# The last two gate cells of a decoder trunk: products in an order of their own, one sum in PSUM, and a closing scale on two engines

## The chip, the cores and the metric

The kernel runs on one core of one Trainium2 chip. The core's engines work side by side, each with its own queue in fixed order: PE (matrix products, with its weight loads beside them), DVE (elementwise), ACT (functions and copies), POOL (small scalar steps here) and SP, which issues the DMAs. The metric is the device time of one execution in microseconds (us), taken as the median of several runs.

## What is computed

The reference is one decoder layer over a sequence of 1024 rows of 1024 columns, in float32, with a gated linear attention branch, a short convolution branch, a merge, an output projection, a gated per-layer embedding and a final norm. The change concerns its end only:

```
ple_gate = sigmoid(rms_norm(x, norm_ple_g) @ w_ple_gate)
x = x + ple_gate * (p @ w_ple_proj)
return rms_norm(x, norm_final_g)
```

The product p @ w_ple_proj is made at the start of the kernel and kept in DRAM (`ped`). The norm ahead of the gate is folded into the weight (its gain) and into the sigmoid's scale (`rgate`, one value per row). So what is left at the end is a matrix product of x with the gate's weight, the sigmoid, a multiplication by `ped`, an addition to x, and the final norm: the mean square of each row, its power of -0.5 (`rf`), and a multiplication by `rf` and by the gain `gf`.

## The kernel before

**Cells.** Every large product is cut into cells. A gate cell `gt0` to `gt3` makes 256 rows of the gate; its operands are halved both ways, and instead of eight products of the halves it makes seven by the Strassen-Winograd scheme (class `Cell`, line 704). Each product is twelve matmuls: four steps of 128 along the inner dimension, and each step three times, since a float32 operand is split into a high and a low part (`mm3`, line 591). A product accumulates in a PSUM bank of 128 x 512. A cell has three banks: X, Y and V. Two cells make a pair, with banks m0 to m2 for the first and m3 to m5 for the second.

With p0 to p6 for the products, the four quarters of a cell's result come out like this (`run`, line 763):

- quarter (0,0) is X = p0 + p3
- Y begins as a copy of p0 (ACT), and becomes U2 = p0 + p2. Product 2 is followed by an ACT copy of Y into SBUF (`c12`)
- V = p1, copied by ACT into SBUF (`c22`)
- quarter (0,1) is V + p5 + c12: product 5 runs on into V, and then DVE adds V and c12 (line 788)
- quarter (1,1) is U2 + p4 + c22: product 4 runs on into Y, then DVE adds Y and c22 (line 792)
- quarter (1,0) is U2 + p4 + p6: product 6 runs on into Y

For the very last cell product 6 is made in two halves of 256 columns (`last_product`, line 748): the first goes on in Y, the second in another bank Z, into which ACT has copied Y before. This lets the first half be read while the second is made. Z is here the X bank of the other cell.

**Order.** A pair takes turns: product 0 of the first cell, product 0 of the second, then 1, 2, 3, 5, 4 and 6 in the same manner (`PAIR`, line 702; `line_up`, line 802). The matmuls of products are put on PE in just this order. `run_groups` (line 816) prepares the streamed operand of a product (`prep`: sums and differences on DVE, the split by an ACT cast and a DVE subtraction) seven products ahead, in a ring of eight buffers, and loads its parts fourteen products ahead.

**The queues.** The program first notes all operations, and a planner (class `Flow`, line 247) then sorts them. `set_dues` gives every operation a due time, counted back from the end with a cost and a latency for each kind of operation. `put_in_order` runs a model of the five queues: at each step it takes the engine that can start soonest, and on it, of the operations that are ready by then, the one with the earliest due. `hurry` moves a due by hand. The order so found is the fixed order of each queue; on the chip an operation that isn't ready holds what stands behind it.

**The end of a gate cell.** `make_gate` (line 1637) says what happens to each quarter. In the usual way (`cons`, line 1688) there are the sigmoid (ACT), the product with `pe` (DVE), the addition to x (DVE) and the mean square (ACT with an accumulator). After both quarters of a row block POOL makes `rf` in two steps, and one DVE operation over 1024 columns multiplies by `rf` and `gf`; one store follows. The second row block of gt2 and of gt3 goes through `piece` (line 1643): the quarter that comes first is already multiplied by `gf`, and when the last piece is there, `rf` is made by an addition on DVE and a power on POOL. Then the first quarter is only scaled by `rf` and stored, and the last one is multiplied by `rf` and `gf` and stored. For gt2 the scale of 512 columns is on DVE; for gt3 512 columns are scaled by ACT and 256 by DVE. All stores are issued by SP. The rows of x that gt2 and gt3 need are loaded into four buffers (tag "x", line 1684) that the row blocks of gt0 and gt1 hold until they are stored.

Of the kernel before, what the change touches and what calls it, by code (L numbers as in the profile page):

```python
# [9 lines left out]
F32 = mybir.dt.float32  # L10
# [6 lines left out]
P = 128  # L17
# [229 lines left out]
class Flow:  # L247
# [12 lines left out]
    def note(self, engine, op, call, args, kw):  # L260
# [12 lines left out]
        for d in shape[1:]:  # L273
            n *= d
        o.lat = 0.15
        if engine == PE:
# [127 lines left out]
    def put_in_order(self):  # L404
# [28 lines left out]
        while len(order) < len(ops):  # L433
            best = None
            for e in range(5):
                found = [(max(clock[e], w), n) for n in waiting[e] for w in [since(ops[n])] if w is not None]
                first = None
                if e == PE and at < len(main) and not ops[main[at]].left:
                    w = since(ops[main[at]])
                    if w is not None:  # L440
                        first = (max(clock[e], w), main[at])
                when = min([w for w, _ in found + ([first] if first else [])], default=None)
                if when is None or best and best[0] <= when:
                    continue
                ripe = [n for w, n in found if w <= when]
                pick = min(ripe, key=lambda n: (ops[n].due + (6.0 if ops[n].table and ops[n].table != table else 0.0), n),
                           default=None)
                best = (when, e, first[1] if pick is None else pick)
            assert best, "nothing can run"
            when, e, n = best  # L450
            o = ops[n]
# [45 lines left out]
BACKLOG = 3.0  # L497
LATE = 2.2
START = 30.0


@with_exitstack
def kernel(
# [195 lines left out]

    ORDER, PAIR = tuple(range(7)), (0, 1, 2, 3, 5, 4, 6)

    class Cell:


        def __init__(self, name, side, src, res, cons, prods=ORDER, begin=None, s1=None, u2=None, s5=None, fresh=()):
            self.name, self.side, self.src, self.res, self.cons = name, side, src, res, cons
            self.prods, self.begin, self.after = list(prods), begin, None
            self.get = {"u2": u2, "s5": s5}  # L710
            self.s1, self.seed, self.ready, self.halves = s1, None, lambda k: True, None
# [11 lines left out]

        def prep(self, k):
            if k not in self.ring:
                self.load(k)
                self.ring[k] = self.steps[k]()

# [18 lines left out]

        def last_product(self):

            other = psm.tile([P, 512], F32, tag=f"m{3 * (1 - self.set)}", name=f"{self.name}Z")  # L750
            nc.scalar.copy(other, self.Y)
            self.prep(6)
            shi, slo = self.ring[6]
            rhi, rlo = self.res[6]
# [8 lines left out]
        def run(self, k):  # L763
            if k == self.prods[0]:
                if self.begin:
                    self.begin()
                self.Y = None
            if k == 0:
                self.X = bank(self, 0)
                self.product(0, self.X, True)  # L770
# [2 lines left out]
            elif k == 1:  # L773
# [3 lines left out]
                self.V = bank(self, 2)  # L777
                self.product(1, self.V, True)
                self.c22 = self.taken("s5", self.V)
            elif k == 2:  # L780
                self.product(2, self.Y, False)
                self.c12 = self.taken("u2", self.Y)
            elif k == 3:
                self.product(3, self.X, False)
                self.cons(0, 0, self.X)
            elif k == 5:
                self.product(5, self.V, False)
                tt(self.c12, self.V, self.c12, op=ALU.add)
# [13 lines left out]
    def line_up(groups):  # L802
        for n, g in enumerate(groups):
            for s, c in enumerate(g):
                c.set = (s if len(g) > 1 else n) % 2
        return [(c, k) for g in groups for k in g[0].prods for c in g]

    def single(cs):
        return [[c] for c in cs]

    def pairs(cs):
        for c in cs:
# [759 lines left out]
    with phase("late", [ph["sw"], ep]) as lp:  # L1572
# [60 lines left out]
        with phase("fin", [ph["sw4"]], lp) as gp:  # L1633
# [3 lines left out]
            def make_gate(p, cell):  # L1637
# [3 lines left out]


                def piece(i, cs, src, n, done):
                    w = cs.stop - cs.start
                    a = cs.start
# [8 lines left out]
                    act(junk[:, 0:w], xc, AF.Square, scale=1.0 / 32.0, accum_out=m)  # L1654
                    if not done:
                        tt(xc, xc, gf[:, cs], op=ALU.mult)
                        pre = gp.tile([P, 1], F32, tag="pre", name=f"pre{p}_{i}_{n}", bufs=4)
# [12 lines left out]
                    if a:  # L1670
                        nc.vector.tensor_scalar(xt[i][:, 0:a], xt[i][:, 0:a], r[:, 0:1], None, op0=ALU.mult)
                    store(out[rows(2 * p + i), 0:512], xt[i][:, 0:512])

                def late_cons(i, j, src):
                    if not xt:
                        get()
                    piece(i, slice(512 * j, 512 * j + 512), src, 1 - j, j == 0)

                def halves(n, src):
                    piece(1, slice(256 * n, 256 * n + 256), src, 1 + n, n == 1)  # L1680
# [25 lines left out]
                cell.cons = cons  # L1706
# [73 lines left out]
```

## Time and profile before

| | |
|---|---|
| median of 3 runs | 1102.06 us (1101.98 to 1102.79) |
| the profiled execution | 1102.23 us |
| its span in the profile | 1100.4 us |
| granted PE clock | 0.998 of full speed |
| instructions | 15273, of them 5050 matmuls |
| PE, DVE, ACT, POOL busy | 99%, 78%, 54%, 5% of the span |

A timeline row has the start in us from the beginning of the span, the duration, the engine, the line of the program, the operation, the tiles (out <- in, without their numbers), the shapes and the count of merged instructions; a bracket at its end gives the idle time before it and what ended that. All lines of computing read L491, since the planner issues everything from there; so tiles tell the steps apart: gt3Y is bank Y of gt3, `junk` the mean square, `pe` the product of gate and embedding, `x` the row block, `rf` the closing factor. In a row of the windows view stand the stretch, its length, and for each engine its busy time and in brackets its instructions (PE, PE's weight loads, DVE, ACT, POOL), then the granted clock, the share of the 16 DMA engines and GB/s. A row of waits has who waited, for whom, the total in us, how often, and the longest.

### The profile page before, as it was taken

The page shows a single profiled execution, that of the slowest core. Times are in us where ns is not written, and L with a number is a line of the kernel's source. Part 1 is how long each engine was busy: PE and PEld are TensorE (multiplying, and loading weights), DVE is VectorE, ACT ScalarE, POOL GpSimd, SP SyncE. Part 2 cuts the span into 40 slices and gives each one's busy share as a digit, 9 for nine tenths or more (in the row PEclk, how much of TensorE's full clock was granted, in tenths as well). Part 3 has the DMA queues.
Part 4 walks back from the last instruction along what each step waited for, and adds up shares of the span by engine and source line. Part 5 has one row for each costly group of instructions (what it writes and reads, how often), then busy time and mean ns, then how long its engine had stood idle before and what let it go on. Part 6 is the DMA issues. An engine that isn't in the chain of part 4 may idle for free.

```text
span 1100.4 us, 15273 instructions
## 1 busy us (share of the span) xinstructions
PE 1089.4 (99%) x5050; PEld 908.3 (83%) x5050; DVE 855.8 (78%) x1386; ACT 598.2 (54%) x1107; POOL 56.0 (5%) x116
## 2 busy tenths in 40 slices
PE   9999999999999999999999999999999999999996
PEld 7888888788888888888888898888888888888885
DVE  6996477789878878748649587876999889868666
ACT  6775347866543554343333377766736445457554
POOL 0000000000000000000000022230000000002021
PEclk9999999999999999999999999999999999999999
DMA  9957463358867595222212699988595888889653
GB/s 317 327 184 246 131 210 109 117 172 252 255 221 268 177 313 180 88 66 66 87 58 65 220 307 345 323 267 293 207 308 176 301 260 291 293 311 320 238 201 114
DMA packets 152574, 238.94 MB, mean 217 GB/s; under 512 B 12976, under 2 KB 66480, under 8 KB 149424
## 3 DMA queue, kind: packets, MB, share of 16 engines
q1 hardware_dynamic: 152496, 237.98, 65.0%
q8 instruction: 39, 0.64, 0.2%
q14 instruction: 39, 0.32, 0.1%
HBM read 157.19 MB, written 80.74 MB: 216 GB/s over the span
## 4 chain that ended last, share of the span: by engine, by line
PE 96%; ACT 2%; DVE 2%; issue 0%; POOL 0%; DVEq 0%; ACTq 0%
PE vacc L491 7%; PE op L491 3%; PE pe L491 2%; PE X L491 2%; PE ga2Y L491 1%; PE ga3Y L491 1%; PE ga1Y L491 1%; PE ga0Y L491 1%; PE out1Y L491 1%; PE gc1Y L491 1%; PE out0Y L491 1%; PE gc0Y L491 1%; PE out3Y L491 1%; PE out2Y L491 1%; PE za0Y L491 1%; PE xc3Y L491 1%
## 5 line engine op out<-in xcount | busy, mean ns | idle before, releaser
L491 ACT ACTIVATE junk<-x 128x512 bf16<-128x512 f32 (+1 forms) x29 | 17.8, 615 | 12.0 <-DVE x L491 11.5
L491 ACT ACT_TABLE_LOAD x17 | 21.8, 1283 | 3.4 <-issue 2.4
L491 DVE TENSOR_TENSOR wt<-wt 128x512 f32<-128x512 f32 x32 | 21.8, 685 | 1.5 <-DMA wtd<-wt 1.3
L491 POOL TENSOR_TENSOR or<-or,mhalf 128x1 f32<-128x1 f32 x32 | 20.4, 638 | 2.7
L491 DVE SCALAR_TENSOR_TENSOR u<-t,vec,u 128x1024 f32<-128x1024 f32 x16 | 20.4, 1276 | 0.0
L491 DVE COPY_PREDICATED aT<-trim,X 128x128 f32<-128x128 int32 x32 | 9.6, 301 | 13.5 <-PE X L491 13.1
L491 POOL MEMSET t<- 128x2 f32 x8 | 0.8, 99 | 378.4 <-DVE u L491 194.8
L491 ACT ACTIVATE og<-op,or 128x256 f32<-128x256 f32 x32 | 15.1, 472 | 8.9 <-POOL or L491 6.5
L491 POOL TENSOR_SCALAR rg<-ms 128x1 f32<-128x1 f32 x8 | 4.9, 612 | 265.8 <-ACT junk L491 265.7
L491 ACT CAST aTh<-aT 128x128 fp32r<-128x128 f32 x32 | 9.5, 298 | 11.4 <-DVE aT L491 9.9
L491 PE MATMUL op<-vl,aTh 128*128 128x256 f32 x64 | 15.0, 314 | 0.0
L491 POOL TENSOR_SCALAR or<-oms 128x1 f32<-128x1 f32 x32 | 8.8, 274 | 119.1 <-ACT junk L491 119.1
L491 PE MATMUL op<-Sh,qkl 128*128 128x256 f32 x56 | 14.6, 283 | 0.0
L491 DVE TENSOR_TENSOR oT<-op,szl 128x256 f32<-128x256 f32 x32 | 13.3, 420 | 0.6 <-DMA od<-oT 0.2
L491 ACT ACTIVATE junk<-op 128x256 bf16<-128x256 f32 x32 | 12.3, 384 | 2.0 <-PE op L491 1.6
L491 DVE TENSOR_TENSOR Sl<-S,Sh 128x256 fp32r<-128x256 f32 x28 | 11.8, 420 | 1.4 <-ACT Sh L491 1.1
L491 PE MATMUL pe<-wpehi,pThi 128*128 128x512 f32 x32 | 12.7, 398 | 0.0
L491 PE MATMUL pe<-wpelo,pThi 128*128 128x512 f32 x32 | 12.6, 393 | 0.0
L491 PE MATMUL pe<-wpehi,pTlo 128*128 128x512 f32 x32 | 12.5, 391 | 0.0
L491 PEld LDWEIGHTS X<-vl,keh 128*128 128x128 f32 x56 | 10.4, 188 | 2.3
L491 PE MATMUL X<-qkl 128*128 128x128 f32 x64 | 12.3, 273 | 0.0
L491 PE MATMUL op<-ident,og 128*128 128x128 f32 x64 | 12.3, 273 | 0.0
(3240 smaller groups left out, 4160.1 us busy)
## 6 DMA issues: line engine op xcount, KB each, us to landing
wtd<-wt SPq DMA_DIRECT2D x44, 256.0 KB, 3.8
qkl<-qkd SPq DMA_DIRECT2D x32, 320.0 KB, 4.9
wt<-in_wb_dram SPq DMA_DIRECT2D x8, 1024.0 KB, 6.5
vl<-vd SPq DMA_DIRECT2D x32, 256.0 KB, 4.8
vraw<-in_wb_dram SPq DMA_DIRECT2D x28, 256.0 KB, 4.4
wgq<-wtd SPq DMA_DIRECT2D x7, 1024.0 KB, 7.3
uq<-ud SPq DMA_DIRECT2D x5, 1024.0 KB, 5.6
oq<-od SPq DMA_DIRECT2D x5, 1024.0 KB, 6.1
```

Of the source, the lines that this page charges most:

```text
L491: o.call(*[place(a) for a in o.args], **{k: place(a) for k, a in o.kw.items()})
```

## The change

It has five parts, all for gt2 and gt3, the last pair.

1. The products of the pair get an order by hand, `CLOSE`: 0, 1, 3, 2 of gt2, then 0 of gt3, then 5, 4 of gt2, 3 of gt3, 6 of gt2, and 2, 1, 4, 5, 6 of gt3. Since gt3's product 2 now comes ahead of its product 1, `prep` prepares both at once.
2. For both cells (`closing`) the sum for quarter (0,1) is made in PSUM before product 5. Where product 1 came first (gt2), DVE writes V = c22 + Y after product 2, and Y is not copied to SBUF; where product 2 came first (gt3), DVE adds c12 to V after product 1. Product 5 then runs on into V, and the quarter is read from V directly.
3. Z lies in the cell's own X bank, and only the half of Y that Z needs is copied, with a due that is 2.5 later.
4. Both row blocks of gt3 and the second of gt2 go through `piece`. For all but the last one `rf`'s addition is on POOL, the scale of the first quarter on ACT, with dues 1.5 earlier. For the last one ACT scales columns 512 to 1023 and itself issues their store; DVE scales columns 0 to 255 first and then multiplies columns 256 to 511, and SP stores the 512 columns.
5. The planner learns a DMA on ACT's queue (cost 0.1). Past 1060 us of its own time, on DVE and ACT, it may leave an engine idle for up to 0.3 us, where an operation with a due at least 0.5 earlier becomes ready in that time.

```diff
+        if engine == ACT and op == "dma_start":
+            o.cost, o.lat = 0.1, 3.0
...
+                if pick is not None and e in (DVE, ACT) and when > NEAR_END:
+                    soon = [(ops[n].due, n, w) for w, n in found
+                            if when < w < when + min(NEAR, ops[pick].cost) and ops[n].due < ops[pick].due - 0.5]
+                    if soon:
+                        best = (min(soon)[2], e, min(soon)[1])
...
+NEAR, NEAR_END = 0.3, 1060.0
...
+    CLOSE = (0, 1, 3, 2, 10, 5, 4, 13, 6, 12, 11, 14, 15, 16)
...
             if k not in self.ring:
+                if k == 2:
+                    self.prep(1)
...
-            other = psm.tile([P, 512], F32, tag=f"m{3 * (1 - self.set)}", name=f"{self.name}Z")
-            nc.scalar.copy(other, self.Y)
+            other = psm.tile([P, 512], F32, tag=f"m{3 * self.set}", name=f"{self.name}Z")
+            nc.hurry = -2.5
+            nc.scalar.copy(other[:, 256:], self.Y[:, 256:])
+            nc.hurry = 0.0
...
                 self.c22 = self.taken("s5", self.V)
+                if self.closing and self.c12 is not None:
+                    tt(self.V, self.V, self.c12, op=ALU.add)
             elif k == 2:
                 self.product(2, self.Y, False)
-                self.c12 = self.taken("u2", self.Y)
+                if self.closing and self.c22 is not None:
+                    tt(self.V, self.c22, self.Y, op=ALU.add)
+                else:
+                    self.c12 = self.taken("u2", self.Y)
...
+            elif k == 5 and self.closing:
+                self.product(5, self.V, False)
+                self.cons(0, 1, self.V)
...
-                    nc.vector.tensor_scalar(r, m, sums[i][:, 0:1], None, op0=ALU.add)
+                    (nc.vector if last else nc.gpsimd).tensor_scalar(r, m, sums[i][:, 0:1], None, op0=ALU.add)
                     nc.gpsimd.tensor_tensor(r, r, mhalf, op=ALU.pow)
-                    if a:
-                        act(xt[i][:, 512:], xt[i][:, 512:], AF.Copy, scale=r[:, 0:1])
-                    else:
-                        nc.vector.tensor_scalar(xt[i][:, 512:], xt[i][:, 512:], r[:, 0:1], None, op0=ALU.mult)
-                    store(out[rows(2 * p + i), 512:], xt[i][:, 512:])
+                    nc.hurry = 0.0 if last else 1.5
+                    if last:
+                        part = xt[i][:, 512:]
+                        act(part, part, AF.Copy, scale=r[:, 0:1])
+                        nc.scalar.dma_start(out[rows(2 * p + i), 512:], part)
+                        part = xt[i][:, 0:256]
+                        nc.vector.tensor_scalar(part, part, r[:, 0:1], None, op0=ALU.mult)
+                        stt(xc, xc, r[:, 0:1], gf[:, cs], op0=ALU.mult, op1=ALU.mult)
+                        store(out[rows(2 * p + i), 0:512], xt[i][:, 0:512])
+                        return
+                    ready = slice(512, D) if a == 0 else slice(0, 512)
+                    act(xt[i][:, ready], xt[i][:, ready], AF.Copy, scale=r[:, 0:1])
+                    store(out[rows(2 * p + i), ready], xt[i][:, ready])
                     stt(xc, xc, r[:, 0:1], gf[:, cs], op0=ALU.mult, op1=ALU.mult)
-                    if a:
-                        nc.vector.tensor_scalar(xt[i][:, 0:a], xt[i][:, 0:a], r[:, 0:1], None, op0=ALU.mult)
-                    store(out[rows(2 * p + i), 0:512], xt[i][:, 0:512])
+                    store(out[rows(2 * p + i), cs], xc)
+                    nc.hurry = 0.0
...
-                    if i == 1 and p >= 2:
+                    if p == 3 or p == 2 and i == 1:
                         return late_cons(i, j, src)
...
-            run_groups(pairs(gts))
+            run_groups(pairs(gts[:2]) + [Closing(gts[2:])])
```

More of the change, by code (lines that the diff above doesn't have):

```diff
@@ L275, in note @@
         o.lat = 0.15
-        if engine == PE:
+        if engine == ACT and op == "dma_start":
+            o.cost, o.lat = 0.1, 3.0
+        elif engine == PE:
             o.cost, o.lat = n / 2400 + 0.0134, 0.22
@@ L710, in __init__ @@
             self.get = {"u2": u2, "s5": s5}
-            self.s1, self.seed, self.ready, self.halves = s1, None, lambda k: True, None
+            self.s1, self.seed, self.ready, self.halves, self.closing = s1, None, lambda k: True, None, False
             self.raw, self.ring = [None] * 4, {}
@@ L766, in run @@
                     self.begin()
-                self.Y = None
+                self.Y = self.c12 = self.c22 = None
             if k == 0:
@@ L805, in line_up @@
                 c.set = (s if len(g) > 1 else n) % 2
-        return [(c, k) for g in groups for k in g[0].prods for c in g]
+        todo = []
+        for g in groups:
+            if isinstance(g, Closing):
+                todo += [(g[k // 10], k % 10) for k in CLOSE]
+            else:
+                todo += [(c, k) for k in g[0].prods for c in g]
+        return todo
     def single(cs):
         return [[c] for c in cs]
+    class Closing(list):
+        pass
     def pairs(cs):
@@ L1643, in piece @@
                 def piece(i, cs, src, n, done):
-                    w = cs.stop - cs.start
-                    a = cs.start
+                    w, a, last = cs.stop - cs.start, cs.start, p == 3 and i == 1
                     if a % 512 == 0:
@@ L1656, in piece @@
                         tt(xc, xc, gf[:, cs], op=ALU.mult)
-                        pre = gp.tile([P, 1], F32, tag="pre", name=f"pre{p}_{i}_{n}", bufs=4)
+                    if not done:
+                        pre = gp.tile([P, 1], F32, tag="pre", name=f"pre{p}_{i}_{n}", bufs=8)
                         nc.vector.tensor_scalar(pre, m, EPS if n == 0 else sums[i][:, 0:1], None, op0=ALU.add)
@@ L1676, in late_cons @@
                         get()
-                    piece(i, slice(512 * j, 512 * j + 512), src, 1 - j, j == 0)
+                    piece(i, slice(512 * j, 512 * j + 512), src, i ^ j, i != j)
                 def halves(n, src):
@@ L1704, in cons @@
                         store(out[rows(2 * p + i), :], xt[i])
-                cell.cons = cons
+                cell.cons, cell.closing = cons, p >= 2
                 if p == 3:
```

## The prediction, as put on record

> **What bounds the kernel now.** I began with the page's busy shares, to see whether any engine leaves room.
>
> ```profile
> PE 1089.4 (99%) x5050; PEld 908.3 (83%) x5050; DVE 855.8 (78%) x1386; ACT 598.2 (54%) x1107; POOL 56.0 (5%) x116
> ```
>
> TensorE (PE) is busy for 1089.4 us, 99% of the span, so a change that keeps the same products can win only where PE is idle. Next I cut the span at the last pair of gate cells and at the last matmul.
>
> ```profile
> 1052.10:1091.03 38.93, 38.89 (x182) 32.22 (x180) 25.98 (x37) 19.89 (x43) 8.10 (x8) 1.00 0.53 189
> 1091.03:1100.40 9.37, 0.00 (x0) 0.00 (x0) 5.51 (x16) 2.87 (x9) 1.48 (x2) 0.71 0.30 112
> ```
>
> The columns after the length are PE, its weight loads, DVE, ACT and POOL. In the last pair PE is never idle for long; after its last matmul 9.37 us pass in which DVE still works 5.51 us. That tail is the stake. The PE timeline says how the pair is paced.
>
> ```profile
> 1074.10 0.39 PE L491 MATMUL gt2V<-wg5hi,gt2hi 128*128 128x512 f32 x1
> ...
> 1076.82 0.39 PE L491 MATMUL gt3V<-wg5hi,gt3hi 128*128 128x512 f32 x1
> ...
> 1087.47 0.39 PE L491 MATMUL gt2Y<-wg6hi,gt2lo 128*128 128x512 f32 x1
> 1087.90 0.39 PE L491 MATMUL gt3Y<-wg6hi,gt3hi 128*128 128x256 f32 x1
> ...
> 1090.75 0.28 PE L491 MATMUL gt3Z<-wg6hi,gt3lo 128*128 128x256 f32 x1
> ```
>
> One product of twelve matmuls takes 1076.82 - 1074.10 = 2.72 us, or 0.227 each. The last product should start at 1087.70 (1087.47 + 0.23) and starts at 1087.90. It is 0.20 late, and the list of waits names the reason: gt3's product 6 follows its product 4 too closely, and DVE has not yet read Y.
>
> ```profile
> PEld gt3Y L491 <- DVE gt3s L491: 0.5, 1, 0.5
> ```
>
> Then the tail itself, first on DVE, then on ACT.
>
> ```profile
> 1093.14 0.42 DVE L491 TENSOR_TENSOR x<-x,pe 128x256 f32<-128x256 f32 x1
> ...
> 1094.20 0.21 DVE L491 TENSOR_SCALAR rf<-msl,pre 128x1 f32<-128x1 f32 x1
> ...
> 1095.13 1.14 DVE L491 SCALAR_TENSOR_TENSOR x<-x,rf,gfin 128x512 f32<-128x512 f32 x2
> 1096.19 0.35 DVE L491 TENSOR_SCALAR x<-x,rf 128x256 f32<-128x256 f32 x1
> ```
>
> ```profile
> 1092.10 0.43 ACT L491 ACTIVATE gt3Z<-gt3Z,rg 128x256 f32<-128x256 f32 x1
> ...
> 1093.66 0.42 ACT L491 ACTIVATE junk<-x 128x256 bf16<-128x256 f32 x1 [0.70 <-DVE x L491]
> 1093.98 0.18 ACT L491 ACTIVATION_READ_ACCUMULATOR junk<-x 128x1 f32 x1
> 1095.29 0.72 ACT L491 ACTIVATE x<-x,rf 128x512 f32<-128x512 f32 x1 [1.12 <-POOL rf L491]
> ```
>
> Z is complete at 1091.03 (1090.75 + 0.28), but its sigmoid starts at 1092.10: ACT and DVE are still finishing gt2's last two quarters. The rest of the last row then ends at 1096.01 on ACT (1095.29 + 0.72) and at 1096.54 on DVE (1096.19 + 0.35). What follows is transfer.
>
> ```profile
> 1095.24 1.97 SPq L491 DMA_DIRECT2D out_dram<-x  x4
> ```
>
> ```profile
> 1096.82 0.39 SPq L491 DMA_DIRECT2D out_dram<-x  x1
> ```
>
> ```profile
> 1096.00:1096.10 0.10, 0.00 (x0) 0.00 (x0) 0.10 (x1) 0.01 (x1) 0.00 (x0) 0.50 0.32 123
> ...
> 1098.80:1098.90 0.10, 0.00 (x0) 0.00 (x0) 0.00 (x0) 0.00 (x0) 0.00 (x0) 0.50 0.38 123
> ```
>
> ```profile
> out_dram<-x SPq DMA_DIRECT2D x1, 256.0 KB, 2.5
> ```
>
> Four stores of 256 KB, gt2's last row and gt3's, are issued one after the other from 1095.24 on, the last at 1096.82. By the slices of 0.1 us their data flow from about 1096.05 to 1098.83: the first bytes come 0.81 after the first issue, and 2.78 us for four is 0.695 us each. The last issue lands 2.5 later, at 1099.3; the span ends 1.1 after that.
>
> **The change, part by part.** *The order on PE.* The fourteen products, their 2.72 us and their number stay. gt2 ends at the ninth place instead of the thirteenth, so its closing row leaves the tail. By places of 2.72, counted back from 1087.70 (the pair starts at 1052.34), gt2's product 6 now runs 1074.10 to 1076.82, and gt3 has 2, 1, 4, 5 and 6 after it. gt3's product 4 fills its place until 1084.98 (its last matmul is through 0.16 later, 0.39 less 0.23), product 5 on V comes between, and product 6 starts at 1087.70.
>
> ```profile
> 1085.18 0.57 ACT L491 COPY gt3Z<-gt3Y 128x512 f32<-128x512 f32 x1 [0.95 <-PE gt3Y L491]
> ```
>
> Here ACT took Y 0.04 after the same product 4 of the old order was through, at 1085.14 (1084.98 + 0.16). In the new order this copy, halved to 256 columns, and DVE's sum out of Y (0.69) have from 1085.14 to 1087.70 for themselves. The 0.20 stall goes: PE ends at 1090.83.
>
> *The second sum in PSUM.* The addition after product 5 becomes one that is made before it: for gt2 after product 2, for gt3 after product 1. The count on DVE is the same, two of 0.69; for gt2 one ACT copy (0.57) is saved, and the chain after product 5 is shorter by one DVE step. The price is that PE now waits for it. For gt3, product 1 ends at 1082.42, product 5 starts at 1084.98: 2.56 us for an ACT copy and a DVE sum, 0.57 + 0.69 and three gaps of 0.04, 1.38 in all. For gt2 the gap is the same. I cost it at nothing; the cover is one product by the other's accumulator, 1.2 us wide. It fails only if ACT or DVE stands on another wait at that moment (rivals).
>
> *The last row's chain.* Its links I take from an undisturbed piece of 512 columns.
>
> ```profile
> 1077.74 0.72 ACT L491 ACTIVATE gt2u<-gt2u,rg 128x512 f32<-128x512 f32 x1 [0.21 <-DVE gt2u L491]
> ```
>
> ```profile
> 1078.50 0.69 DVE L491 TENSOR_TENSOR pe<-gt2u,pe 128x512 f32<-128x512 f32 x1 [0.79 <-ACT gt2u L491]
> 1079.22 0.69 DVE L491 TENSOR_TENSOR x<-x,pe 128x512 f32<-128x512 f32 x1
> ```
>
> The gaps are 0.04 from ACT to DVE (1078.46 to 1078.50) and 0.03 on DVE; from DVE to the square it is 0.10 in the tail above (1093.56 to 1093.66). With the 256-column durations: sigmoid 1090.87 to 1091.30, product to 1091.76, sum to 1092.21, square with its read (1093.66 to 1093.98 + 0.18, so 0.50) 1092.31 to 1092.81, rf 1092.85 to 1093.06. The power on POOL has these rows:
>
> ```profile
> 1080.83 0.30 POOL L491 TENSOR_SCALAR rf<-ms 128x1 f32<-128x1 f32 x1 [19.19 <-ACT junk L491]
> 1081.21 0.56 POOL L491 TENSOR_TENSOR rf<-rf,mhalf 128x1 f32<-128x1 f32 x1
> ...
> 1093.77 1.48 POOL L491 TENSOR_TENSOR rf<-rf,mhalf 128x1 f32<-128x1 f32 x2 [7.84 <-DVE rf L491]
> ```
>
> Some 0.08 after its input (1081.13 to 1081.21) it starts and takes 0.56: 1093.14 to 1093.70. From 1093.74 ACT scales 512 columns until 1094.46 (0.72), and DVE scales 256 (0.35) and multiplies 256 (0.42) until 1094.5. That is the bare chain; now DVE ends at 1096.54.
>
> *What lies beside it.* gt3's own first row now closes here too: product 5 ends at 1087.86, its square about 1090.85, then an addition on POOL, a power, an ACT scale (0.72), a DVE multiply of 512 (0.7) and two stores. Between 1085.2 and 1093 DVE has six operations of 0.69, five of 0.42 and three small ones of some 0.2, about 6.8 us for 7.8 us, so it is nearly full. The crowding costs from 0 (everything in gaps) to 0.8 (one DVE multiply of the first row ahead of rf and a held power). The nearest row is the pair of powers at 1093.77, run beside a full DVE: 1.48 for two, 0.36 over twice 0.56. So I take 0.4: DVE ends at 1094.9, ACT at 1094.86.
>
> *The closing stores.* SP issued 0.28 after DVE's end (1096.54, 1096.82); that gives 1095.2, and about 1095.0 for the one issued by ACT. Before shows no DMA issued by ACT: I take SP's 0.33 to 0.39 for the issue; at twice that it costs 0.4 more, and issued side by side it could save 0.3. Two stores from 1095.0: first bytes 0.81 later, 1.39 for two, 1097.2; landing 0.5 after the last byte (1098.83, 1099.3), 1097.7; the end 1.1 later, 1098.8. Gain **1.6 us** of 1100.4. The first row's pair, issued near 1093.5, has flowed by then.
>
> [...]
>
> *What else moves.* gt2's second row now closes between 1077 and 1084 with one ACT scale in place of a DVE one and two stores on SP, past the loads of gt3's last quarters; PE covers it, and those loads are wanted only from 1085 on. gt3's operands for product 1 are prepared along with product 2's, the same casts and subtractions seven places ahead of their use, covered by some 19 us of products. gt2's first two products want their operands 2.7 us earlier, with the same lead. The planner's waiting rule acts only in DVE's and ACT's queues near the end. Outside the tail PE idles 1100.4 - 1089.4 - 9.4 = 1.6 us in all, so a reordering there can win little; I cost it at nothing, between -0.3 and +0.3.
>
> The profiled execution took 1102.23 for its span of 1100.4; the median of the runs is 1102.06. 1102.06 - 1.6 gives **1100.5**, a gain of 0.15%.
>
> **The rivals.** *POOL is held.* The addition that makes r moves from DVE to POOL for gt2's second row; gt3's first row has it there already, but now in the tail.
>
> ```profile
> 1055.74 2.60 POOL L491 TENSOR_SCALAR rf<-ms 128x1 f32<-128x1 f32 x1 [7.56 <-ACT junk L491]
> ```
>
> The row quoted above took 0.30; this one, while DVE multiplied two whole rows, took 2.60. For gt3's first row it starts at about 1090.95, in the thick of DVE's work. At 2.60 it ends at 1093.55, the power at 1094.2; DVE's multiply of that row stands ahead of rf, rf slips to 1094.9, and the last scale ends near 1096.4: gain 0.2. At half of that delay rf slips by about 1.0 over the bare chain: gain 1.0. The middle, 0.6, gives **1101.5**. Against it: DVE's products out of PSUM come between, and the POOL row at 1080.83 shows how short a gap is enough. [...]
>
> *PE stalls at the PSUM sum: slower.* gt2's product 3 now ends at 1060.66 and not at 1071, but its row x must first be loaded into a buffer that gt0's stored row frees.
>
> ```profile
> 1060.77 1.51 SPq L491 DMA_DIRECT2D x<-x2d  x1
> ```
>
> ```profile
> x<-x2d SPq DMA_DIRECT2D x1, 512.0 KB, 6.4
> ```
>
> It lands at 1067.2 (1060.77 + 6.4). If the planner puts gt2's addition to x ahead of the sum c22 + Y on DVE, that sum waits from 1063.4 until 1067.9 and ends at 1068.6, where product 5 wanted it by 1065.94: PE loses 2.7 us, and the time is 1102.06 - 1.6 + 2.7 = **1103.2**. It decides from a stall of 1.6 us on. Against it: the planner counts stores and loads, and must misjudge this one by over 2 us.
>
> *The bare chain.* No crowding, an ACT store that runs beside SP's: 0.4 + 0.3 more, a gain of 2.2 to 2.3, **1099.8**. It needs every gap to fall right.
>
> *The edits don't bite.* The order on PE is written out, so that rival is empty for the products; for the stores it is the case of ACT's issue at twice the price, inside the range.
>
> **How the numbers follow.** Forecast 0.58, POOL 0.22, stall 0.08, bare chain 0.12. A measurement of this kernel tells about 0.2%, 2.2 us, from no change. Faster by that: the bare chain, 0.12. Slower by that, above 1104.3, needs a stall of 3.8 us, a later landing than that row's: 0.05 of the 0.08. Within 0.2%: 0.83. The range takes the forecast with its unknowns (crowding -0.4 to +0.4, the ACT issue -0.3 to +0.4, upstream 0.3: 1099.7 to 1101.5) and POOL's worst case (gain 0.2 is 1101.9): **1099.7 to 1101.9**.
>
> **What would show it.** Right: the last matmul 0.2 earlier and no wait of PE at gt3Y; Z's sigmoid within 0.1 of that end; DVE's last row near 1094.9; the last two stores issued within 0.4 of each other; a tail of 8 us. Wrong: a POOL addition over 1 us near 1091 and rf behind it; a wait of PE for a DVE sum into gt2V or gt3V; an ACT store that lands over 3 us after its issue.

## The result, and the profile after

The changed kernel takes 1100.9 us in the median of 17 runs (1100.06 to 1102.21), the kernel before 1102.4 in the median of 17 runs beside it (1101.79 to 1103.47). The ratio is 0.9985, with a 95% interval of 0.9979 to 0.9992: a gain of 1.65 us by the ratio, where 1.6 was forecast. The profiled execution took 1100.47 for a span of 1098.4.

The page's busy shares of the changed kernel answer to the first line shown of before.

```profile
PE 1089.0 (99%) x5050; PEld 908.0 (83%) x5050; DVE 856.5 (78%) x1386; ACT 599.0 (55%) x1108; POOL 54.2 (5%) x117
```

The same matmuls, the same count on DVE. So I cut the span as in the prediction: the last pair of cells up to PE's last matmul, and the tail. The columns after the length are PE, weight loads, DVE, ACT and POOL with their instructions, then the granted clock.

```profile
1052.20:1090.60 38.40, 38.40 (x181) 32.11 (x179) 27.73 (x44) 20.17 (x43) 6.46 (x8) 1.00 0.51 182
1090.60:1098.40 7.80, 0.00 (x0) 0.00 (x0) 3.49 (x11) 2.75 (x9) 1.93 (x3) 0.68 0.36 134
```

The tail is 7.80 where it was 9.37: 1.57 of the 2.0 by which the span is shorter. The other 0.43 is PE's end, 1090.60 where it was 1091.03. The PE timeline of the changed kernel splits it.

```profile
1052.20 0.39 PE L498 MATMUL gt2X<-wg0hi,gt2hi 128*128 128x512 f32 x1
...
1084.85 0.39 PE L498 MATMUL gt3V<-wg5hi,gt3hi 128*128 128x512 f32 x1
...
1087.57 0.28 PE L498 MATMUL gt3Y<-wg6hi,gt3hi 128*128 128x256 f32 x1
...
1090.32 0.28 PE L498 MATMUL gt3Z<-wg6hi,gt3lo 128*128 128x256 f32 x1
```

The pair starts 0.14 earlier (1052.20 for 1052.34). Product 6 starts 2.72 after product 5, one product's length: the stall of 0.20 is gone, and no row of waits names gt3Y. From product 6's first matmul to its last there are 2.75 us where there were 2.85. Now the tail of the changed kernel, on DVE, ACT and POOL.

```profile
1090.65 0.68 DVE L498 TENSOR_TENSOR x<-x,gfin 128x512 f32<-128x512 f32 x1
1091.25 0.42 DVE L498 TENSOR_TENSOR pe<-gt3Z,pe 128x256 f32<-128x256 f32 x1
...
1092.18 0.75 DVE L498 SCALAR_TENSOR_TENSOR x<-x,rf,gfin 128x512 f32<-128x512 f32 x1
1092.85 0.21 DVE L498 TENSOR_SCALAR rf<-msl,pre 128x1 f32<-128x1 f32 x1
1092.98 0.41 DVE L498 TENSOR_TENSOR x<-x,gfin 128x256 f32<-128x256 f32 x1
...
1094.10 0.48 DVE L498 SCALAR_TENSOR_TENSOR x<-x,rf,gfin 128x256 f32<-128x256 f32 x1
```

```profile
1090.63 0.45 ACT L498 ACTIVATE gt3Z<-gt3Z,rg 128x256 f32<-128x256 f32 x1
...
1092.55 0.19 ACT L498 ACTIVATION_READ_ACCUMULATOR junk<-x 128x1 f32 x1
1092.64 0.70 ACT L498 ACTIVATE x<-x,rf 128x512 f32<-128x512 f32 x1
1093.83 0.72 ACT L498 ACTIVATE x<-x,rf 128x512 f32<-128x512 f32 x1 [0.49 <-POOL rf L498]
1094.58 0.39 ACTq L498 DMA_DIRECT2D out_dram<-x  x1
```

```profile
1090.79 0.71 POOL L498 TENSOR_SCALAR rf<-msl,pre 128x1 f32<-128x1 f32 x1 [9.93 <-ACT junk L498]
1091.58 0.57 POOL L498 TENSOR_TENSOR rf<-rf,mhalf 128x1 f32<-128x1 f32 x1
1093.14 0.66 POOL L498 TENSOR_TENSOR rf<-rf,mhalf 128x1 f32<-128x1 f32 x1 [0.99 <-DVE rf L498]
```

Z's sigmoid follows PE's end by 0.03, where it was 1.07. DVE is through at 1094.58 (1094.10 + 0.48), 3.98 after PE's end; before it was 5.51 (1096.54 - 1091.03). Last the stores, from SP's queue (all three, then the last alone) and from the DMA issues of the tail.

```profile
1092.96 1.98 SPq L498 DMA_DIRECT2D out_dram<-x  x3
```

```profile
1094.61 0.33 SPq L498 DMA_DIRECT2D out_dram<-x  x1
```

```profile
out_dram<-x ACTq DMA_DIRECT2D x1, 256.0 KB, 2.8
out_dram<-x SPq DMA_DIRECT2D x1, 256.0 KB, 2.6
```

The next line has what the DMA engines moved in 40 slices of 0.15 from 1092.0 to 1098.0.

```profile
GB/s 0 0 0 0 0 0 0 0 0 0 0 14 341 382 410 396 342 382 423 369 355 82 41 314 396 410 396 355 382 410 396 314 82 0 0 0 0 0 0 0
```

The first row's two stores are issued from 1092.96 on and have flowed by 1095.3, before the last row's two begin to flow. Before, four stores were issued from 1095.24 to 1096.82. Yet the stretch behind DVE is hardly shorter for it: from DVE's end to the end of the span there are 3.82 (1098.40 - 1094.58), before 3.86 (1100.40 - 1096.54). So 1.53 of the 1.57 is DVE's earlier end.

### The profile page after: what moved, and what is told of

It is laid out like the page before. It is cut to its first block, busy times and chain, and to the rows that moved or that the text cites. A ratio compares the mean times of both kernels' runs of the same rounds, so it can differ in the third digit from the quotient of the medians.

```text
span 1098.4 us, 15282 instructions
## 1 busy us (share of the span) xinstructions
PE 1089.0 (99%) x5050; PEld 908.0 (83%) x5050; DVE 856.5 (78%) x1386; ACT 599.0 (55%) x1108; POOL 54.2 (5%) x117
## 4 chain that ended last, share of the span: by engine, by line
PE 98%; ACT 1%; DVE 1%; issue 0%; POOL 0%; POOLq 0%; DVEq 0%; ACTq 0%
PE vacc L498 7%; PE op L498 3%; PE pe L498 2%; PE X L498 2%; PE ga2Y L498 1%; PE ga3Y L498 1%; PE ga1Y L498 1%; PE ga0Y L498 1%; PE out1Y L498 1%; PE gc1Y L498 1%; PE out0Y L498 1%; PE gc0Y L498 1%; PE out2Y L498 1%; PE out3Y L498 1%; PE za0Y L498 1%; PE ya3Y L498 1%
## 5 line engine op out<-in xcount | busy, mean ns | idle before, releaser
L498 ACT ACTIVATE wt<-wt,vec 128x512 f32<-128x512 f32 x16 | 10.7, 717 | 4.2 <-DMA zc1raw<-in_wc_dram 2.4
```

Source lines behind the costliest of these rows:

```text
L498: o.call(*[place(a) for a in o.args], **{k: place(a) for k, a in o.kw.items()})
```

## The experiments

In several of these profiles PE has one more wait, of 0.4 to 1.5 us, at a tile far upstream that the change doesn't touch. The changed kernel shows none in the profile above, and here it is on another execution of the very same kernel, in the run named "changed again":

```profile
PEld xc1Y L498 <- ACT xc1u L498: 1.1, 1, 1.1
```

Since it comes and goes with one and the same kernel, I compare the tails from each profile's own last matmul, not the ends of PE. The two profiles of the changed kernel have tails of 7.80 and 7.83. The ratios are to the kernel before, run on the same chip. Each tail is read from one execution, and the intervals of the ratios reach some 0.7 to 1.0 us to either side, so most of the shares below are seen in the tails alone; the ratios rank the kernels nearly as the tails do.

| run | ratio (95%) | tail, us |
|---|---|---|
| before | 1 | 9.37 |
| changed | 0.9985 (0.9979 to 0.9992) | 7.80 |
| the order alone | 1.001 (1.0001 to 1.0018) | 10.68 |
| all but the order | 0.9991 (0.9982 to 0.9999) | 8.48 |
| no sum in PSUM | 0.9992 (0.9983 to 1.0001) | 8.71 |
| last store from SP | 0.9985 (0.9976 to 0.9994) | 7.77 |
| first row the old way | 0.9989 (0.998 to 0.9998) | 8.32 |
| no waiting rule | 0.9983 (0.9974 to 0.9992) | 7.96 |
| last product 384 + 128 | 0.9984 (0.9975 to 0.9993) | 7.54 |
| changed again | 0.9987 (0.9978 to 0.9996) | 7.83 |

### Which part shortens the tail

The first theory was that the order does it, by taking gt2's closing row out of the tail. The order alone, put into the kernel before:

```diff
+    CLOSE = (0, 1, 3, 2, 10, 5, 4, 13, 6, 12, 11, 14, 15, 16)
...
+                if k == 2:
+                    self.prep(1)
...
-            run_groups(pairs(gts))
+            run_groups(pairs(gts[:2]) + [Closing(gts[2:])])
```

> The kernel before with the order of the fourteen products alone. The order theory (the gain comes from gt2's closing work leaving the tail, and from the 0.2 us stall of PE) expects PE to end 0.2 to 0.4 earlier with no wait at gt3Y, and a tail from PE's end to the end of the span of 8.4 to 8.9 us, where before has 9.4 and the changed kernel 7.8: gt3's first row still closes with a DVE multiplication of 1024 columns (1.28 us) and a DVE sum (0.69) after product 5, both in the tail. Gain 0.6 to 1.2 us of the changed kernel's 1.5. The closing theory (the gain comes from how the last rows are closed: sum in PSUM, scale on ACT, a store from ACT) expects no gain: within 0.3 us of before.

Its tail is the longest of all, 10.68, and the ratio is above 1. The theory fell, and that the kernel would be slower than before neither theory had expected. On PE the order does what it should: the pair takes 38.39 from its first matmul to PE's end, where before it took 38.69 (1091.03 - 1052.34). The tail of this run, on DVE, ACT and POOL:

```profile
1094.81 1.28 DVE L491 SCALAR_TENSOR_TENSOR x<-x,rf,gfin 128x1024 f32<-128x1024 f32 x1
```

```profile
1096.52 0.72 ACT L491 ACTIVATE x<-x,rf 128x512 f32<-128x512 f32 x1 [1.88 <-POOL rf L491]
```

```profile
1094.97 1.52 POOL L491 TENSOR_TENSOR rf<-rf,mhalf 128x1 f32<-128x1 f32 x1 [0.28 <-DVE rf L491]
```

Then SP's queue (all three stores, then the second alone), SP's wait, and the DMA issue of the 512 KB:

```profile
1097.27 1.30 SPq L491 DMA_DIRECT2D out_dram<-x  x3
```

```profile
1097.65 0.43 SPq L491 DMA_DIRECT2D out_dram<-x  x1
```

```profile
SPq L491 <- ACT x L491: 12.9, 1, 12.9
```

```profile
out_dram<-x SPq DMA_DIRECT2D x1, 512.0 KB, 2.9
```

gt2's row is gone from the tail, but gt3's first row has taken its place, and it closes late: as in the kernel before, its quarter (0,1) needs a sum after product 5, and then one multiplication of 1024 columns. DVE's end stays where it was relative to PE's (1097.28 - 1091.72 = 5.56 for 5.51). What is worse is the stores: the first is issued 5.55 after PE's end, where it was 4.21 (1095.24 - 1091.03), and the same 1 MB has yet to flow. That difference, 1.34, is about the 1.31 by which the tail is longer.

Part of this is the order on SP's queue and not that of the products. The first row's multiplication ends at 1096.09 (1094.81 + 1.28), but its store of 512 KB is issued only at 1097.65: on SP's queue a store of the last row stands ahead of it and waits until ACT's scale ends at 1097.24. In the run with the first row the old way, below, the same store follows its multiplication by 0.02 (1094.96 after 1094.94). An estimate from the prediction's terms, 0.81 to the first bytes, 0.695 for each 256 KB and 1.6 from the last byte to the end: issued at 1096.1, the store would leave a tail of some 9.6. The order alone would then cost 0.2 and not 1.3, and would still gain nothing in the tail. No run tests this.

The opposite, the changed kernel with the pair's usual order:

```diff
-            run_groups(pairs(gts[:2]) + [Closing(gts[2:])])
+            run_groups(pairs(gts))
```

> The changed kernel with the old order of turns. The order theory expects gt2's second row to close in the tail again, beside both rows of gt3: a tail of 9.0 to 9.8 us, PE waiting about 0.2 us at gt3Y, and a time within 0.4 us of before. The closing theory expects a tail near 8 us and at least 1.0 us of the gain.

The closings alone bring 0.89 of tail (9.37 to 8.48), between the ranges of the two theories; the order on top of them brings 0.68 more. The order's worth has the other sign with and without the closings, though by the estimate above SP's queue makes most of the loss without them. That the order pays only when the row that it puts last but one closes early fits these runs, and is argued. This run has no wait of PE at gt3Y either, and neither has the order alone; the pair takes 38.39 in both. So either is enough to remove that stall; that the halved copy into Z does it here is only argued.

The changed kernel without the sums in PSUM:

```diff
-                cell.cons, cell.closing = cons, p >= 2
+                cell.cons, cell.closing = cons, False
```

> The changed kernel with quarter (0,1) summed by DVE after product 5 again. The order theory, with DVE nearly full from 1085 to 1093, expects the sum of 0.69 us to push gt3's first row and, through DVE's queue, the last row by 0.3 to 0.7 us: tail 8.1 to 8.5. If DVE had room, as the rival says, the tail stays within 0.1 of 7.8. PE has no new wait in either case.

0.91 of the tail is the sum's, more than the 0.3 to 0.7 expected. After product 5 DVE makes it beside the last row's links, the first row's multiplication slips behind `rf`, and the power beside it is held. DVE first, then POOL:

```profile
1094.77 0.21 DVE L498 TENSOR_SCALAR rf<-msl,pre 128x1 f32<-128x1 f32 x1
1094.90 0.74 DVE L498 SCALAR_TENSOR_TENSOR x<-x,rf,gfin 128x512 f32<-128x512 f32 x1
```

```profile
1095.07 0.99 POOL L498 TENSOR_TENSOR rf<-rf,mhalf 128x1 f32<-128x1 f32 x1 [0.32 <-DVE rf L498]
```

Next, the first row of gt3 closed in the old way, with one multiplication over 1024 columns and one store, all else as changed:

```diff
-                    if p == 3 or p == 2 and i == 1:
+                    if i == 1 and p >= 2:
                         return late_cons(i, j, src)
```

> The changed kernel, but gt3's first row closes in the old way: its mean square is closed after both quarters, and one multiplication over 1024 columns follows. Theory A (the early closing of that row keeps a long DVE operation out of the last row's chain): the multiplication by rf over 1024 columns, 1.28 long in the run with the order alone, stands on DVE ahead of the last row's addition or beside its power, so the last power ends 0.6 to 1.1 later, the tail after PE's last matmul grows from 7.8 to between 8.4 and 9.0, and the time is some 0.6 to 1.1 over the changed kernel's. Rival B (the row only fills gaps of DVE, and the gain is all from the sum in PSUM and the shared scale): tail within 0.2 of 7.8.

The tail grows by 0.52, a little under theory A's range, and rival B's bound of 0.2 is passed. The multiplication stands where theory A had it:

```profile
1093.66 1.28 DVE L498 SCALAR_TENSOR_TENSOR x<-x,rf,gfin 128x1024 f32<-128x1024 f32 x1
1094.86 0.20 DVE L498 TENSOR_SCALAR rf<-msl,pre 128x1 f32<-128x1 f32 x1
```

`rf` starts 2.98 after PE's end (1094.86 - 1091.88), where it was 2.25. The power behind it takes 0.55 again, so part of that comes back.

Two parts weigh little or nothing. The last 512 columns stored by SP:

```diff
-                        nc.scalar.dma_start(out[rows(2 * p + i), 512:], part)
+                        nc.note(ACT, "dma_start", tc.nc.sync.dma_start, (out[rows(2 * p + i), 512:], part), {})
```

> The changed kernel with the same order of all queues, but the store of columns 512 to 1023 of the last row issued by SP, not by ACT. If a second issuer saves issue time alone, the two issues now stand 0.4 us apart instead of side by side, and the last landing moves by 0.0 to 0.4 us: tail 7.8 to 8.2. If ACT's queue brought transfers of its own beside SP's, the tail would grow by about half of the two transfers' 1.39 us, 0.7 us or more.

The tail is 7.77 for 7.80. And the waiting rule off:

```diff
-NEAR, NEAR_END = 0.3, 1060.0
+NEAR, NEAR_END = 0.0, 1060.0
```

> The changed kernel with the planner's waiting rule of 0.3 us switched off, so that DVE and ACT near the end take the operation that is ready first. Theory A (the rule is a detail of the order near the end): tail within 0.3 of 7.8 and a time within 0.4 of the changed kernel's. Rival B (the rule is what keeps long operations of the other row out of the last row's chain): an operation of gt3's first row stands ahead of one of the last row's links, and the tail is 8.3 to 8.8.

The tail is 7.96, 0.16 more, and the ratio that of the changed kernel within its interval: theory A, a detail of the order. No run takes out ACT's scale of the first quarters alone, or the halved copy into Z alone.

### A version with a smaller last piece

```diff
-            nc.scalar.copy(other[:, 256:], self.Y[:, 256:])
+            nc.scalar.copy(other[:, 384:], self.Y[:, 384:])
...
-                cs = slice(n * 256, n * 256 + 256)
+                cs = slice(384 * n, 384 + 128 * n)
...
-                    piece(1, slice(256 * n, 256 * n + 256), src, 1 + n, n == 1)
+                    piece(1, slice(384 * n, 384 + 128 * n), src, 1 + n, n == 1)
```

DVE's first scale goes from 256 to 384 columns as well.

> The changed kernel with gt3's last product cut into 384 and 128 columns in place of 256 and 256. PE's work is the same (the last four steps are shorter but more is done before). Theory (the last row's chain from PE's end is sigmoid, product, sum and square of the last piece, so a piece of half the width saves part of each of the four): each link is about 0.1 to 0.15 shorter by the difference of the rows for 512 and 256 columns (ACT 0.66 to 0.45, DVE 0.69 to 0.42), 0.4 to 0.5 in all, of which DVE's first scale, now 384 wide, gives back about 0.1: tail 7.4 to 7.6. Rival (matmuls of 128 columns are paced by their weight loads, so PE ends later; or DVE is full of the first row's operations in that stretch and the chain can't use the shorter links): tail or PE's end takes it back, time as changed or up to 0.4 longer.

Theory and rival were both right. The tail is 7.54, as the theory has it. But PE's last product is longer, as the rival has it:

```profile
1087.80 0.33 PE L498 MATMUL gt3Y<-wg6hi,gt3hi 128*128 128x384 f32 x1
...
1089.97 0.27 PE L498 MATMUL gt3Z<-wg6lo,gt3hi 128*128 128x128 f32 x1
...
1091.08 0.28 PE L498 MATMUL gt3Z<-wg6hi,gt3lo 128*128 128x128 f32 x1
```

From its first matmul to its last there are 3.28 us for 2.75. The ten steps from 1089.97 to 1091.08 are 0.111 apart, and those of 256 columns were 0.12 apart: half the columns save next to nothing. In all 0.53 lost on PE and 0.26 won in the tail; the ratio, 0.9984, can't be told from the changed kernel's. No version here beats the changed kernel by more than can be measured.

### What the slower rival would have cost

In the changed kernel the rival's order did come about: the addition of gt2's row stands directly ahead of the sum in PSUM.

```profile
1062.95 0.68 DVE L498 TENSOR_TENSOR x<-x,pe 128x512 f32<-128x512 f32 x1
1063.55 0.69 DVE L498 TENSOR_TENSOR gt2V<-gt2s,gt2Y 128x512 f32<-128x512 f32 x1
```

What did not come about is the late load. The planner moved it up:

```profile
1056.34 0.37 SPq L498 DMA_DIRECT2D x<-x2d  x1
```

```profile
x<-x2d SPq DMA_DIRECT2D x1, 512.0 KB, 3.5
```

Issued 4.4 earlier than in the kernel before, the row lands at 59.84 past 1000, some 3.1 before DVE takes it up at 1062.95. The sum is done at 1064.24, 1.57 before product 5 starts at 1065.81. So the load could be some 4.7 later before PE waits. To price the wait I issued this load again into the same buffer: three times in full, twice and a half, and twice and three quarters. Nothing is left out. The edit of the first, with the planner told of one load only (for the others the third has `[:, 0:512]` or `[:, 0:768]`):

```diff
-                        load(xt[i], x2d[2 * p + i])
+                        if p == 2 and i == 0:
+                            nc.note(SP, "dma_start", lambda *v: [tc.nc.sync.dma_start(*v) for _ in range(3)],
+                                    (xt[i], x2d[2 * p + i]), {})
+                        else:
+                            load(xt[i], x2d[2 * p + i])
```

> The changed kernel, but the load of gt2's first row of x is issued three times, into the same buffer from the same rows; nothing is left out. In the changed kernel this row lands at 59.8 after 1000, the addition to it stands on DVE right ahead of gt2's sum in PSUM, and product 5 of gt2 starts at 1065.8. Two more loads of 3.5 each move the landing to about 1066.9, the sum's end to 1068.3. Theory (what stands in DVE's queue ahead of a PSUM sum decides whether PE stalls, and the cover is the gap up to product 5): PE waits 2 to 3 us at gt2's bank V, and the time is 2 to 3 us over the changed kernel's, near 1103.3. Rival (the three loads overlap on the DMA engines or the planner's order lets DVE go on): no wait of PE at that bank, time as changed.

> The changed kernel with gt2's first row of x loaded twice in full and once by half into the same buffer (1.75 in the time of one load of 3.5 for the last part); nothing is left out. By the run with three loads, where the row's addition on DVE started at 1067.70 and PE waited 2.88, half a load less brings the sum's end 1.7 earlier: PE waits some 1.1 us at bank V. Theory (only a wait of about 3 us makes the chip grant half the clock afterwards): the granted clock stays at 1.00 after it, product 5 takes its 2.72, and PE's end is only the 1.1 later; time near 1102.2. Rival (any wait of this kind costs in addition): the twelve matmuls of product 5 take over 4 us again, time near 1103.9.

> As the run beside it, but the third load is three quarters of the row. PE should wait some 2.0 us at bank V. [...]

> The changed kernel itself, for comparison on the same chip: no wait of PE at gt2's bank V, PE's end near 1090.6, span 1098.4, tail 7.8, time within 0.5 of 1100.9.

| loads | PE idle at gt2's product 5 | product 5, first matmul to product 4's first | pair's first matmul to PE's end | median, us | ratio (95%) |
|---|---|---|---|---|---|
| 1 (changed; changed again) | 0 | 2.72 | 38.40 | 1101.35 | 0.9987 (0.9978 to 0.9996) |
| 2 1/2 | 1.65 | 2.87 | 40.36 | 1103.12 | 1.0003 (0.9994 to 1.0013) |
| 2 3/4 | 2.40 | 4.36 | 42.68 | 1105.18 | 1.0019 (1.0008 to 1.0029) |
| 3 | 2.88 | 4.44 | 43.20 | 1104.79 | 1.0019 (1.001 to 1.0028) |

The times of the first row are those of the run named "changed again", the stretches those of the first profile; the run with three loads was made on another chip than the other three, with its own runs of before. The three waits, in the PE timelines of two and a half, two and three quarters, and three loads:

```profile
1067.51 0.50 PE L498 MATMUL gt2V<-wg5hi,gt2hi 128*128 128x512 f32 x1 [1.65 <-DVE gt2V L498]
```

```profile
1069.31 0.50 PE L498 MATMUL gt2V<-wg5hi,gt2hi 128*128 128x512 f32 x1 [2.40 <-DVE gt2V L498]
...
1070.69 0.63 PE L498 MATMUL gt2V<-wg5hi,gt2lo 128*128 128x512 f32 x1
```

```profile
1069.05 0.50 PE L498 MATMUL gt2V<-wg5hi,gt2hi 128*128 128x512 f32 x1 [2.88 <-DVE gt2V L498]
```

And why the last two cost more than their wait: the granted clock, the third number from the end, around the wait with two and three quarters of loads, then with three, and then with two and a half.

```profile
1066.00:1070.30 4.30, 1.90 (x9) 1.27 (x8) 2.12 (x4) 1.49 (x4) 0.00 (x0) 1.00 1.00 384
1070.30:1073.70 3.40, 3.40 (x10) 2.57 (x9) 0.47 (x1) 0.44 (x2) 0.00 (x0) 0.52 0.91 248
```

```profile
1070.00:1071.00 1.00, 1.00 (x4) 0.72 (x3) 0.52 (x1) 0.27 (x1) 0.00 (x0) 0.50 1.02 369
...
1072.00:1073.00 1.00, 1.00 (x3) 0.78 (x3) 0.00 (x0) 0.00 (x0) 0.00 (x0) 0.51 0.88 270
```

```profile
1068.00:1069.00 1.00, 1.00 (x6) 0.78 (x5) 0.74 (x2) 0.73 (x2) 0.00 (x0) 1.00 0.88 338
1069.00:1070.00 1.00, 1.00 (x6) 0.82 (x5) 0.00 (x0) 0.00 (x0) 0.00 (x0) 1.00 0.78 238
```

After an idle time of 2.40 PE ran at 1.00 for about a microsecond and then for 3.4 us at half, when only nine matmuls began where fifteen would have (3.4 / 0.227). Product 5 took 4.36 in place of 2.72: 1.6 us on top of the wait. After 2.88 idle it is the same, with 1.7 on top (4.44). After 1.65 idle the profile shows no such stretch (1.00 in each of the four slices of 1 us from 1067 on). The two waits came 0.4 to 0.55 longer than I had expected. After the shorter the clock stayed at 1.00, as the theory had it. After the longer it went to half, which speaks against the theory that it takes a wait of about 3 us. Each of the three waits is one execution, so what sets those of 2.40 and 2.88 apart from that of 1.65, their length or also when they fall, stays open. The runs of two and a half loads spread from 1102.0 to 1106.4, so some of the executions without a profile may have been hit as well.

## Why the prediction was right, point by point

**PE's stall at gt3Y, -0.20.** Measured -0.19: of the 0.43 by which PE ends earlier, 0.14 came from upstream, inside the ±0.3 allowed for it, and 0.10 from product 6 itself. Its first two matmuls start 0.11 apart (1087.57, 1087.68); before, where the first came out of a wait, they stood 0.22 apart (1087.90, 1088.12). That last bit was not in the forecast. The forecast also drew this gain from the new order together with the halved copy; the runs show that the order alone, or the closings alone, give PE as much.

**The sum in PSUM, costed at nothing.** Right: no wait of PE at gt2V or gt3V. gt3's sum is the tighter one by its rows:

```profile
1082.94 0.70 DVE L498 TENSOR_TENSOR gt3V<-gt3V,gt3u 128x512 f32<-128x512 f32 x1 [1.30 <-ACT gt3s L498]
```

It is through at 1083.64, 1.2 before product 5 at 1084.85, the forecast's cover to the tenth. But the forecast gave this edit only a shorter chain after product 5, in half a sentence, and no number. Taking it out costs 0.91, the largest single share found.

**gt2's closing row leaves the tail.** True, and by itself it shortens nothing: with the order alone the tail is 1.3 longer, in part by SP's queue. The forecast had said that gt3's first row closes here too, and put it under crowding; what it didn't say is that the order depends on the other parts. Its sum was right because it costed the whole change's end state from PE's end on, and not the difference part by part. That the median's gain came within 0.05 of the forecast is luck in part: 0.24 of PE's earlier end was in no term, and the wait upstream comes and goes by 0.4 to 1.5.

**The bare chain, and 0.4 of crowding.** The bare chain is 3.67 (1090.83 to 1094.5), DVE's end came 3.98 after PE's, so the crowding is 0.31. It can be read off the rows above. DVE's product with `pe` waits for a multiplication by the gain and starts at 1091.25, 0.62 after the sigmoid's start, where the bare chain has 0.47: 0.15. `rf` starts at 1092.85, 0.11 after the square's read (1092.55 + 0.19) where a gap is 0.04: 0.07, behind the first row's multiplication at 1092.18. The power takes 0.66 for 0.56: 0.10. That is 0.32.

**The closing stores.** Forecast for 1095.0 and 1095.2, they are issued at 1094.58 by ACT and at 1094.61 by SP. That is 0.03 after DVE's end, where the forecast took 0.28 from before; there SP was still issuing the third store until 1096.73. The landing after 2.8 and 2.6 is near the forecast's 2.7 and 2.5, and from DVE's end to the end of the span there are 3.82, where 3.9 were forecast. The ACT issue takes 0.39, near SP's 0.33, and saves nothing (the tail is 7.80, and 7.77 with SP alone). The bytes of the last two stores flow in some 1.4 us in both runs, from 1095.4 to 1096.85 with ACT's issue and in ten slices of 0.14 with SP alone, near the forecast's 1.39 (twice 0.695). The tail as a whole was forecast at 7.97 (1090.83 to 1098.8) and is 7.80. The median of the runs lies 0.4 above the forecast, and the runs of before beside it lie 0.3 above the three it was reckoned from.

**The rival of the held POOL, 0.22.** Its order of events happened: the first row's addition starts at 1090.79 in the thick of DVE's work, and DVE's multiplication of that row stands ahead of `rf`. Its price didn't: the addition took 0.71, not 2.60 or half of it, and `rf` slipped by 0.07, not 1.0. It ended at 1091.50, 0.17 after DVE's multiplication by the gain (1090.65 + 0.68), while DVE was at the product out of gt3Z from 1091.25 on. The addition of 2.60 in the kernel before had ended at 1058.34, 0.17 after the last of three operations that DVE ran beside it without a gap:

```profile
1057.49 0.68 DVE L491 TENSOR_TENSOR x<-x,pe 128x512 f32<-128x512 f32 x1
```

**The rival of the PE stall, 0.08.** The order happened, the late load didn't. The prediction's point of decision was a stall of 1.6 us. The run with 1.65 stands at a ratio of 1.0003, and that point agrees. Beyond it the price was wrong. A stall of 2.7 was given 2.7; the runs with 2.40 and 2.88 lost 4.3 and 4.8 from the pair's start to PE's end (42.68 and 43.20 for 38.40); of that 1.6 and 1.7 are the product at the lower clock. Had the rival come, the time by these runs would have been near 1105 and not 1103.2, an estimate.

**The bare chain as a rival, 0.12.** It needed every gap to fall right and an ACT store beside SP's. Crowding of 0.31 and a store that saves nothing speak against it.

## What to carry to other kernels

Cost the last stretch from its own bound, link by link from PE's end to the last byte, and not as a sum of what each edit removes: here one edit made the tail 0.7 shorter or 1.3 longer by what stood beside it. When an order moves one piece of work out of the tail, look what moves in, and whether its stores are issued before the last ones, which a store that isn't ready can hold up on its queue (by 1.56 with the order alone, 1097.65 for 1096.09). A sum that PE must wait for is free as long as it ends before the product that runs on into its bank; a load that it stands behind counts too. Where PE would stand idle, look at the granted clock behind the wait as well: here the waits of 2.40 and 2.88 cost 1.6 and 1.7 more at half the clock, and after the one of 1.65 it stayed at 1.00.

## What the runs showed of the hardware

**A power on POOL beside DVE's multiplication of a row by the gain.** In three runs the last power began while DVE was at that multiplication. DVE's operation ended at 1096.09 (order alone), 1095.64 (no sum in PSUM), 1093.39 (changed), the power at 1096.49, 1096.06 and 1093.80, each 0.40 to 0.42 later, whether it took 1.52, 0.99 or 0.66. With DVE idle (1095.06 to 1095.72) the same instruction took 0.55, in the run with the first row the old way:

```profile
1095.14 0.55 POOL L498 TENSOR_TENSOR rf<-rf,mhalf 128x1 f32<-128x1 f32 x1 [1.72 <-DVE rf L498]
```

and 0.55 in the run without the waiting rule, with DVE idle from 1093.49 to 1094.15. In the kernel before it took 0.56 from 1047.62, beside DVE's sum out of the bank gt1Y (1047.28 to 1047.97). A power that had started first was not held: the changed kernel's first one took 0.57 from 1091.58, though DVE's addition of `pe` to `x` ran from 1091.71. So what such a step cost in these runs can be read off DVE's queue.

**The clock after a short idle time.** 2.40 us of idle PE were followed by 3.4 us at half the clock (0.52 from 1070.30 to 1073.70), and 2.88 us by 0.50 to 0.51 in the slices from 1070 to 1073; 1.65 us were not, in the execution profiled (1.00 from 1067 to 1071).

**Matmuls of 128 columns.** They started 0.111 apart, those of 256 columns 0.12 apart. In the kernel before, matmuls of a single column (`ms<-ones,sq`, fifteen from 18.99 on) start 0.111 apart too, as do their weight loads (fifteen in 1.75 from 18.89 on, the last of 0.19), which fits the rival's pace by the weight loads.
